# Queries and keys of three branches with stationary weights, differential values first, one division on VectorE: a hybrid encoder trunk on one core

## The chip, the cores and the metric

One core of a Trainium2 chip runs the whole program in one launch. The metric is the device time of one execution in microseconds (us). TensorE is PE in the profile, its weight load PEld, VectorE DVE, ScalarE ACT, GpSimd POOL and SyncE SP.

## The reference, cut

Two layers work on x of 256 tokens by 1024. One projection of the normalised x gives the inputs of four branches: a (mLSTM, 4 heads of 128, with a short convolution on queries and keys), b (grouped-query attention, 8 heads, 2 key heads), c (neighbourhood attention, 8 heads) and d (differential attention, 4 heads with two score maps each). A gated sum goes through an output projection, and a SwiGLU feed-forward network (FFN) of width 2816 follows.

```python
def hybrid_layer(x, ...):
    h = rms_norm(x, norm1_g)
    proj = jnp.einsum('bsd,de->bse', h, w_in)
    (aq, ak, av, ao, ag, bq, bk, bv, cq, ck, cv, dq, dk, dv, gl) = jnp.split(proj, points, axis=-1)
    y_a = mlstm_branch(aq, ak, av, ao, ag, a_conv_w, a_gate_bias, a_norm_g)
    y_b = gqa_branch(bq, bk, bv, b_qnorm_g, b_knorm_g)
    y_c = natten_branch(cq, ck, cv, c_rpb)
    y_d = diff_branch(dq, dk, dv, d_lq1, d_lk1, d_lq2, d_lk2, d_subln_g, lambda_init)
    g = jax.nn.sigmoid(gl.astype(F32)).reshape(bsz, s, N_BRANCH, D_MODEL)
    merged = (g[:, :, 0] * (y_a @ w_up_a) + g[:, :, 1] * (y_b @ w_up_b)
              + g[:, :, 2] * (y_c @ w_up_c) + g[:, :, 3] * (y_d @ w_up_d))
    x = x + merged.astype(dt) @ w_out
    h2 = rms_norm(x, norm2_g)
    ffn = (jax.nn.silu(h2 @ w_ffn_gate) * (h2 @ w_ffn_up)) @ w_ffn_down
    return x + ffn
```

## The kernel before, in words

**Arithmetic.** Every large product is three matmuls: operands are split into a high part (fp32r) and a low part (the rest), and high x high, high x low and low x high are summed in PSUM. `mm3` issues the three.

**Weights.** They come in units of two halves. A half is 128 partitions by 1024 columns (512 KB) and lies in one of four buffers `raw`. ACT copies its high part into one of five buffers `whi` (`emit_hi`), DVE subtracts to get the low part into `wlo` (`emit_lo`), and the next load is issued. `need_half(h, live)` makes sure that half h is converted before a block uses it; `live` is the oldest half still in use, and a conversion goes at most five halves beyond it.

**Blocks.** The list `PLAN` names the blocks of a layer in order: `d0 d1` (queries and keys of branch d, two heads' worth each), `a0 a1` and `c0 c1` alike, `dv av cv` values, `bkv` and `bq` for branch b, `ao` the output gate of a, `gXn` and `uXn` the merge gate and the up-projection of branch X, column half n. Nearly all of them go through `in512` and `blk512`: the transposed activations `xT` are stationary (128 tokens), 512 columns of weights move, and two token halves t use two of the three dense PSUM banks `pd`. So a block wants a half, does 12 matmuls with it (two t, two k tiles of 128, three products), and goes on to the next. `tok_evac` copies a finished bank to SBUF on ACT with the token's norm factor as scale per partition (`rc`, `r8`: columns of the statistics tile `st`). Since that result has tokens on partitions and the attention wants head dimensions there, `a_head` (one per head of a) and `soft_item` (one per pair of heads of b, c, d) first transpose it on PE, in four transposes for a, c and d (two for b), into a bank `pa` of five.

```python
            PS.put(p)
            yield
            while not (PS.ok(2) and W2.ok(2) and SM.ok(1) and B["ready"](i)):
                yield
            ps, e, sm = (PS.get(), PS.get()), (W2.get(), W2.get()), SM.get()
```

**Order.** Nothing is scheduled on the chip. `slot`, called between the matmul groups of a block, decides what is put next into the queues of the other engines: first evacuations (`later`), then conversions, then steps of the tasks (`a_head`, `soft_item` and others), as long as DVE and ACT are not more than `FILL` = 2.5 us ahead of PE by the planner's own costs (`Meter.cost`, `Track`). `until` holds the emission of a block up until a condition is met. So a changed block changes the place of conversions and small work in all queues.

**End of the FFN.** Of the last two units of the down projection, column chunk 0 is done for both t with both units, then chunk 1 (`pairs`, in the loop near the end of `trunk`); in the last layer the last quarter goes through `last_block` in two pieces of 256 columns.

Other names: `K4`, `W2`, `SM`, `RQ`, `RE`, `YT`, `T2`, `EA` are pools of tiles (k, w, sm, rq, re, yt, t, acc in the rows); `Res.ok(n)` asks for n free ones.

Of the kernel before, what the change touches and what calls it, by code (L numbers as in the profile page):

```python
# [15 lines left out]
ALU = mybir.AluOpType  # L16
# [21 lines left out]
PLAN = ("d0 d1 dv bkv a0 a1 av bq gd0 gd1 ud0 ud1 c0 c1 cv gb0 gb1 ub0 ub1 "  # L38
# [132 lines left out]
def trunk(ctx: ExitStack, tc, x_in, wts, par, parc, cst, dist, t2w, fg, out):  # L171
# [56 lines left out]
    mvt = sb("mvt", [128, 16])  # L228

    with tc.manual_schedule():  # L230
# [268 lines left out]
        bnd = {"i": 0, "sq": 0, "done": set()}  # L499
# [23 lines left out]
        def square(t, c, st):  # L523
            w = W2.get()
            A.activation(w[:, :512], x[:, t, c * 512:(c + 1) * 512], AF.Square,
                         accum_out=st[:, 2 * c + t:2 * c + t + 1])
            W2.put(w)
            bnd["sq"] += 1
            if bnd["sq"] % 4 == 0:
                V.tensor_tensor(st[:, 4:6], st[:, 0:2], st[:, 2:4], op=ALU.add)  # L530
                V.tensor_scalar(st[:, 4:6], st[:, 4:6], 1.0 / D, EPS, op0=ALU.mult, op1=ALU.add)
                rsq(st[:, 6:8], st[:, 4:6], 2)
                V.tensor_scalar(st[:, 8:10], st[:, 6:8], 0.5, None, op0=ALU.mult)
                V.tensor_tensor(st[:, 10:12], st[:, 6:8], st[:, 8:10], op=ALU.mult)
                for i in range(5):
                    V.tensor_scalar(st[:, 12 + 2 * i:14 + 2 * i], st[:, 6:8], 0.125 * 4 ** i, None, op0=ALU.mult)
# [128 lines left out]
        def a_head(B, h, pc):  # L665

            while not ("t%d" % (h // 2) in B and B["fly"] < 2 and PS.ok(1) and W2.ok(3)):
                yield
            B["fly"] += 1
            tok = B["t%d" % (h // 2)]  # L670
            p, xp, cv, th = PS.get(), W2.get(), W2.get(), W2.get()
# [4 lines left out]
            if h % 2 == 1:  # L676
                B["freet%d" % (h // 2)]()
            xv_ = xp[:, :512].rearrange("p (i n) -> p i n", i=2)
            yield
            A.activation(xp[:, :512], p, AF.Copy)  # L680
# [3 lines left out]
            for i in (0, 1):  # L684
                A.activation(cs_[i], p[:, i * 256:(i + 1) * 256], AF.Identity, scale=taps[i][1])
            PS.put(p)
# [11 lines left out]
            W2.put(xp, th)  # L698
# [101 lines left out]
        def soft_item(B, i, kind):  # L800
# [3 lines left out]
            while not (B["src"](i) is not None and PS.ok(1) and RQ.ok(1)):  # L804
                yield
            qs, ks, free = B["src"](i)
            p, r = PS.get(), RQ.get()
            for t in (0, 1):
                T.transpose(p[:, tsl(t)], qs(t), ident)
                if ks is not None:  # L810
                    T.transpose(p[:, 256 + t * 128:256 + (t + 1) * 128], ks(t), ident)
            free()
            n = 256 if ks is None else 512
            yield
            A.activation(r[:, 0, :n], p[:, :n], AF.Copy)
            yield
            sub_lo(r[:, 1, :n], p[:, :n], r[:, 0, :n])
            PS.put(p)
# [42 lines left out]
            if kind != "d":  # L861
                for c in (0, 1):
                    e3 = e[c][:, :512].rearrange("p (t n) -> p t n", t=2)
                    G.tensor_tensor(e3, e3, rz[:, 2 * c:2 * c + 2].unsqueeze(2).to_broadcast([128, 2, 256]),
                                    op=ALU.mult)
# [92 lines left out]
        def pair_src(B):  # L958

            def src(i):  # L960
                tl = B.get("t%d" % (i // 2))
                if tl is None:
                    return None

                def free():
                    B["used"] = B.get("used", 0) + 1
                    if B["used"] in (2, 4):
                        B["freet%d" % (B["used"] // 2 - 1)]()
                o = (i % 2) * 128
                return (lambda t: tl[:, t, o:o + 128]), (lambda t: tl[:, t, 256 + o:256 + o + 128]), free  # L970
            return src

        def d_main(l, B):
            li = 0.8 - 0.6 * math.exp(-0.3 * l)
            B["src"] = pair_src(B)
# [16 lines left out]
            while "t0" not in B:  # L992
                yield
# [20 lines left out]
        def b_main(B):  # L1014
# [53 lines left out]
            def src(i):  # L1068
# [3 lines left out]
                return (lambda t: qt_[:, t * 512 + i * 128:t * 512 + (i + 1) * 128]), None, free  # L1072
# [8 lines left out]
        def c_main(l, B):  # L1081
            B["t2"] = {}
            B["done"] = 0
            B["src"] = pair_src(B)
            B["ready"] = lambda i: i in B["t2"] and "vr" in B
            B["v"] = lambda kt, i, c: vc[:, kt, 2 * i + c]
            while "t0" not in B or not yt_ok("c"):
                yield
# [23 lines left out]
        for l in range(L):  # L1112
# [5 lines left out]
            r8 = lambda t, i=0, st=st: st[:, 12 + 2 * i + t:13 + 2 * i + t]  # L1118

            def tok_evac(B, key, tl=None, halves=False, early=False):  # L1120
                if tl is None:
                    res = EA if early else K4
                    until(lambda: res.ok(1))
                    raw_ = res.get()
                    B["free" + key] = lambda: res.put(raw_)
                    tl = raw_ if early else raw_.rearrange("p (t n) -> p t n", t=2)
# [3 lines left out]
                def done(t, p):  # L1130
                    if halves:
                        if B is Bd:

                            for i in (0, 1):
                                A.activation(tl[:, t, tsl(i)], p[:, tsl(i)], AF.Identity,
                                             scale=r8(t, 2 * int(key[1]) + i + 1))
                        else:
                            A.activation(tl[:, t, 0:256], p[:, 0:256], AF.Identity, scale=r8(t))
                        A.activation(tl[:, t, 256:512], p[:, 256:512], AF.Identity, scale=rc(t))
                    else:  # L1140
                        A.activation(tl[:, t, :], p, AF.Identity, scale=rc(t))
# [118 lines left out]
            for n in PLAN:  # L1260
                if n in start:
                    start[n]()
                if l == 0 and n == PLAN[0]:
                    first_block(tok_evac(Bs[n[0]], "t" + n[1], halves=n[0] != "a", early=n[0] != "c"),
                                pc[:, C_G1:C_G1 + 8])
# [8 lines left out]
                else:  # L1274
                    in512(n, tok_evac(Bs[n[0]], "t" + n[1], halves=n[0] != "a", early=n[0] != "c"))
# [147 lines left out]
            for c, t, un, j in ([(0, t, *q) for q in pairs for t in (0, 1)] + [(1, t, *q) for t in (0, 1) for q in pairs]):  # L1423
# [129 lines left out]
```

## Time and profile before

| | before |
|---|---|
| runs, median (lowest to highest) | 1070.75 us (1070.56 to 1071.57), 3 runs |
| the profiled execution, its own time | 1070.18 us |
| its span | 1068.4 us |
| granted TensorE clock, mean | 0.999 |
| matmuls on PE | 5270 |
| weight halves of 1024 columns (512 KB) | 331 loads |

The span is what the profiler saw between the first and last instruction; the execution's own time is 1.8 us longer. In the table of windows each stretch shows the busy time of every engine and, in brackets, its instructions; in a timeline the first number is the start from the span's start, the second the duration of the row, and x the instructions in it. Matmuls overlap, so the distance of two starts, and not the duration, tells what a matmul costs PE.

### The profile page before, as it was taken

Reading aid. Unit: us, or ns where it says so; the run is one execution under the profiler, and the core shown is the slowest. Engines: PE = TensorE matmul, PEld = TensorE weight load, DVE = VectorE, ACT = ScalarE, POOL = GpSimd, SP = SyncE. Lnnn points to the kernel's source line nnn. Section 1 sums busy time; section 2 is a strip of 40 time slices with the busy share of each in tenths; the row PEclk is TensorE's granted clock in tenths of the full one; section 3 lists DMA queues with packets and bytes.
Section 4 is the critical chain, followed back from the end, with each engine's and each line's share of the span. In section 5 each row is a group of like instructions: output and inputs, shape, how many; then the busy total and the mean of one; then the engine's idle time right before and its main releaser. Section 6 shows DMA issues by size and latency. Waiting matters only on the chain.

```text
span 1068.4 us, 14722 instructions
## 1 busy us (share of the span) xinstructions
PE 1055.5 (99%) x5270; PEld 876.2 (82%) x5270; DVE 760.6 (71%) x1356; ACT 617.3 (58%) x1091; POOL 156.3 (15%) x130
## 2 busy tenths in 40 slices
PE   9999999999999999999999999999999999999997
PEld 7888887888888888888788888788888888888885
DVE  5889798788656755565576989987975666556555
ACT  6766658775444544444468656687744464444443
POOL 0010345143300000000000006434223000000000
PEclk9999999999999999999999999999999999999999
DMA  8355434445555564555544444355465555564551
GB/s 300 122 178 176 158 134 155 161 146 188 191 181 169 197 203 171 197 185 185 185 160 143 164 168 150 126 169 170 136 199 194 181 172 202 174 210 164 197 191 65
DMA packets 53001, 184.80 MB, mean 173 GB/s; under 512 B 6081, under 2 KB 7489, under 8 KB 52929
## 3 DMA queue, kind: packets, MB, share of 16 engines
q1 hardware_dynamic: 50256, 178.33, 49.6%
q10 hardware_dynamic: 2672, 5.55, 1.7%
q8 instruction: 41, 0.67, 0.2%
q14 instruction: 32, 0.25, 0.1%
HBM read 182.80 MB, written 1.05 MB: 172 GB/s over the span
## 4 chain that ended last, share of the span: by engine, by line
PE 93%; DVE 5%; ACT 1%; issue 1%; DMA 0%; POOLq 0%; POOL 0%; DVEq 0%; ACTq 0%
PE pd L166 66%; PE pa L166 27%; DVE wlo L166 1%; DVE w L166 1%; DVE sm L166 1%; ACT w L166 1%; DVE k L166 1%; DMA x<-in_x_dram 0%; DVE rq L166 0%; ACT whi L166 0%; ACT yt L166 0%; DVE acc L166 0%; DVE yt L166 0%; ACT pa L166 0%; DVE x L166 0%
## 5 line engine op out<-in xcount | busy, mean ns | idle before, releaser
L166 PE MATMUL pd<-whi,xT 128*128 128x512 f32 (+1 forms) x1952 | 623.9, 391 | 0.0
L166 DVE TENSOR_TENSOR wlo<-raw,whi 128x1024 fp32r<-128x1024 f32 (+2 forms) x344 | 424.1, 1244 | 104.3 <-ACT whi L166 103.1
L166 ACT ACTIVATE whi<-raw 128x1024 fp32r<-128x1024 f32 (+2 forms) x344 | 354.6, 1040 | 140.2 <-PE pd L166 106.6
L166 PEld LDWEIGHTS pd<-whi,xT 128*128 128x128 f32 x1952 | 364.9, 188 | 74.0
L166 PE MATMUL pd<-wlo,xT 128*128 128x512 f32 (+1 forms) x976 | 377.6, 387 | 0.3 <-DVE wlo L166 0.3
L166 PEld LDWEIGHTS pd<-wlo,xT 128*128 128x128 f32 x976 | 183.5, 188 | 35.3 <-DVE wlo L166 1.4
L166 PE MATMUL pa<-whi,yt 128*128 128x512 f32 x408 | 137.0, 397 | 1.4 <-ACT yt L166 1.4
L166 PEld LDWEIGHTS pa<-whi,yt 128*128 128x128 f32 x408 | 76.5, 188 | 18.1 <-ACT yt L166 1.9
L166 PE MATMUL pd<-whi,yt 128*128 128x512 f32 (+1 forms) x272 | 86.2, 386 | 0.0
L166 PE MATMUL pa<-wlo,yt 128*128 128x512 f32 x204 | 79.5, 390 | 0.0
L166 POOL TENSOR_TENSOR st<-st,mhalf 128x2 f32<-128x2 f32 (+1 forms) x6 | 3.9, 656 | 513.9 <-DVE st L166 513.9
L166 DVE SCALAR_TENSOR_TENSOR w<-w,pd 128x256 f32<-128x256 f32 x44 | 18.6, 423 | 83.0 <-ACT w L166 82.8
L166 ACT ACTIVATE k<-pd,st 128x512 f32<-128x512 f32 (+1 forms) x52 | 31.6, 626 | 53.2 <-PE pd L166 53.0
L166 PEld LDWEIGHTS pd<-whi,yt 128*128 128x128 f32 x272 | 50.6, 188 | 9.7
L166 ACT ACTIVATE w<-pd,st 128x256 f32<-128x256 f32 (+1 forms) x48 | 23.7, 493 | 51.6 <-PE pd L166 51.6
L166 PE MATMUL pd<-wlo,yt 128*128 128x512 f32 (+1 forms) x136 | 52.2, 384 | 0.0
L166 ACT ACTIVATE yt<-pa 128x512 fp32r<-128x512 f32 x34 | 20.3, 598 | 55.0 <-PE pa L166 54.9
L166 PEld LDWEIGHTS pa<-wlo,yt 128*128 128x128 f32 x204 | 38.4, 188 | 7.3
L166 POOL TENSOR_TENSOR w<-w,sm 128x512 f32<-128x512 f32 x32 | 39.5, 1257 | 30.6 <-DVE sm L166 30.6
L166 POOL TENSOR_TENSOR acc<-acc,k 128x512 f32<-128x512 f32 x16 | 31.7, 1982 | 80.3 <-DVE k L166 80.3
L166 ACT ACTIVATE w<-w,sm 128x256 f32<-128x256 f32 x64 | 31.8, 502 | 14.8 <-DVE sm L166 9.4
L166 DVE TENSOR_TENSOR yt<-pa,yt 128x512 fp32r<-128x512 f32 x30 | 20.7, 690 | 27.0 <-ACT yt L166 26.9
(156 smaller groups left out, 1025.5 us busy)
## 6 DMA issues: line engine op xcount, KB each, us to landing
raw<-in_wts_dram SPq DMA_DIRECT2D x331, 512.0 KB, 3.7
t<-in_t2w_dram ACTq DMA_DIRECT2D x8, 384.0 KB, 3.6
raw<-in_wts_dram SPq DMA_DIRECT2D x8, 272.0 KB, 3.3
x<-in_x_dram ACTq DMA_DIRECT2D x4, 256.0 KB, 6.0
pt<-in_par_dram SPq DMA_DIRECT2D x1, 584.0 KB, 6.0
pt<-in_par_dram ACTq DMA_DIRECT2D x1, 584.0 KB, 5.0
out_dram<-k SPq DMA_DIRECT2D x2, 288.0 KB, 2.1
raw<-in_wts_dram SPq DMA_DIRECT2D x2, 256.0 KB, 4.7
```

The lines of the kernel that those rows point to most:

```text
L166: return f(out, *a, **k)
```

## The change

- `dv` is moved ahead of `d0 d1` in `PLAN`, and the five scaled copies of the norm factor leave `st` (five small products on DVE a norm).
- The blocks `d0 d1 a0 a1 c0 c1` go through a new `qk_block`: weights are stationary (128 columns), all 256 tokens of `xT` move, so the result has head dimensions on partitions. Four column groups (0, 2, 1, 3) run one after another, each over all eight k tiles; DVE writes the finished group to SBUF, multiplied by a row of norm factors (`rrow`, made once a norm by two matmuls in `row_scale`).
- `a_head` and `soft_item` of c and d lose their four transposes and read that tile. `soft_item` of b keeps two.
- The division by the softmax sum of branch b goes from POOL (two products of 512) to DVE (four of 256). Branch c's stays on POOL.
- At the end of the FFN chunk (1, 0) is put ahead of the last unit of chunk 0.

```diff
-PLAN = ("d0 d1 dv bkv a0 a1 av bq gd0 gd1 ud0 ud1 c0 c1 cv gb0 gb1 ub0 ub1 "
+PLAN = ("dv d0 d1 bkv a0 a1 av bq gd0 gd1 ud0 ud1 c0 c1 cv gb0 gb1 ub0 ub1 "
...
-                for i in range(5):
-                    V.tensor_scalar(st[:, 12 + 2 * i:14 + 2 * i], st[:, 6:8], 0.125 * 4 ** i, None, op0=ALU.mult)
+                if bnd["i"] % 2 == 1:
+                    tasks.append(row_scale(st))
...
+            for t in (0, 1):
+                T.matmul(p[:, tsl(t)], st[:, 6 + t:7 + t].to_broadcast([128, 128]), ident, start=True, stop=True)
+            yield
+            A.activation(rrow, p[:, 0:S], AF.Copy)
+            PS.put(p)
+            bnd["row"] = bnd["i"]
...
-            while not ("t%d" % (h // 2) in B and B["fly"] < 2 and PS.ok(1) and W2.ok(3)):
+            while not (h in B and B["fly"] < 2 and W2.ok(2)):
...
-            for i in (0, 1):
-                for t in (0, 1):
-                    o = i * 256 + (h % 2) * 128
-                    T.transpose(p[:, i * 256 + t * 128:i * 256 + (t + 1) * 128], tok[:, t, o:o + 128], ident)
...
+            if kind == "b":
...
+            else:
+                while not (i in B and RQ.ok(1)):
+                    yield
+                (qk, free), r = B[i], RQ.get()
+                A.activation(r[:, 0, :], qk, AF.Copy)
+                yield
+                sub_lo(r[:, 1, :], qk, r[:, 0, :])
+                free()
...
+                    for qt in (0, 1):
+                        q2 = slice(qt * 256, (qt + 1) * 256)
+                        V.tensor_scalar(e[c][:, q2], e[c][:, q2], rz[:, 2 * c + qt:2 * c + qt + 1], None, op0=ALU.mult)
...
+            def qk_block(n):
...
+                def done(col, p):
+                    i, k = col % 2, col // 2
+                    item = 2 * int(n[1]) + i
+                    o = tl[:, i, k * S:(k + 1) * S]
+                    f = 1.0 if k else {"a": 1.0, "c": 0.125, "d": 0.125 * 4.0 ** (item + 1)}[n[0]]
+                    if f == 1.0:
+                        V.tensor_tensor(o, p[:, 0:S], rrow, op=ALU.mult)
+                    else:
+                        V.scalar_tensor_tensor(o, p[:, 0:S], f, rrow, op0=ALU.mult, op1=ALU.mult)
...
+                u0, u1 = Unit("in", n, 0), Unit("in", n, 1)
+                for ci, col in enumerate((0, 2, 1, 3)):
+                    p = bank()
+                    for kt in range(8):
+                        if kt % 2 == 0:
+                            need_half(2 * u0.u + kt // 2, 2 * u0.u + (kt // 2 if ci == 3 else 0))
+                        for t in (0, 1):
+                            x_ready(t, kt // 4)
+                        w = (u0, u1)[kt // 4].get(kt % 4 * 512 + col * 128, 128)
+                        T.matmul(p[:, 0:S], w[0], xT[:, 0, kt, :], start=kt == 0, stop=False)
+                        T.matmul(p[:, 0:S], w[0], xT[:, 1, kt, :], start=False, stop=False)
+                        T.matmul(p[:, 0:S], w[1], xT[:, 0, kt, :], start=False, stop=kt == 7)
+                        if kt == 7:
+                            until(lambda: bnd["row"] == bnd["i"])
+                            later(lambda col=col, p=p: done(col, p))
+                        if kt % 4 == 3:
+                            slot()
...
-                    in512(n, tok_evac(Bs[n[0]], "t" + n[1], halves=n[0] != "a", early=n[0] != "c"))
+                    qk_block(n)
...
-            for c, t, un, j in ([(0, t, *q) for q in pairs for t in (0, 1)] + [(1, t, *q) for t in (0, 1) for q in pairs]):
+            for c, t, un, j in ([(c, t, *pairs[0]) for c, t in ((0, 0), (0, 1), (1, 0))]
+                                + [(c, t, *pairs[1]) for c, t in ((0, 0), (0, 1), (1, 0))] + [(1, 1, *q) for q in pairs]):
```

In the rows that follow, `whi_72` to `whi_76` and `wlo_77` to `wlo_81` are the five buffers of the weight ring, `raw_111` to `raw_114` the four raw ones; `pd` are dense banks, `pa` the other PSUM banks, `rq` query tiles and `kb` keys of branch b, `k`, `w` and `sm` pool tiles, `acc` the merged sum.

PE at the start of `c0` in layer 0, as it was: one half (`whi_76`, `wlo_81`) is used for both t before the next, and score products of branch b lie between.

```order
L166 MATMUL pd_61<-whi_75,yt_83 128x512
L166 MATMUL pd_62<-whi_76,xT 128x512
L166 MATMUL pd_62<-wlo_81,xT 128x512
L166 MATMUL pd_62<-whi_76,xT 128x512 x2
L166 MATMUL pd_62<-wlo_81,xT 128x512
L166 MATMUL pd_62<-whi_76,xT 128x512
L166 MATMUL pa_64<-kb,rq_87 128x256
L166 MATMUL pd_63<-whi_76,xT 128x512
L166 MATMUL pa_65<-ident,k_1_99 128x128 x2
L166 MATMUL pd_62<-whi_72,xT 128x512
```

PE at the same place now: the end of `ud1`, then the first column group of `c0`.

```order
L166 MATMUL pd_63<-whi_75,yt_83 128x512
L166 MATMUL pd_61<-xT,whi_76 128x256 x2
L166 MATMUL pd_61<-xT,wlo_81 128x256
L166 MATMUL pd_61<-xT,whi_76 128x256 x2
L166 MATMUL pd_61<-xT,wlo_81 128x256
L166 MATMUL pd_61<-xT,whi_72 128x256 x2
L166 MATMUL pd_61<-xT,wlo_77 128x256
L166 MATMUL pd_61<-xT,whi_73 128x256 x2
L166 MATMUL pd_61<-xT,wlo_78 128x256
L166 MATMUL pd_61<-xT,whi_74 128x256 x2
L166 MATMUL pd_61<-xT,wlo_79 128x256
L166 MATMUL pa_67<-ident,k_1_99 128x128 x2
```

The first column group reads four halves (76, 72, 73, 74) one after another, and the second begins again with `whi_76`; before, the second half was read only after both t of the first.

DVE around the same place, as it was (`mvt` and `bsm` belong to branch b's normalisation).

```order
L166 TENSOR_SCALAR k_2_100<-k_2_100,mvt,sm_123 128x128 x4
L166 TENSOR_TENSOR wlo_79<-raw_114,whi_74 128x1024
L166 TENSOR_SCALAR k_2_100<-k_2_100,mvt,sm_123 128x128 x4
L166 TENSOR_REDUCE sm_124<-pa_67 128x2
L166 SCALAR_TENSOR_TENSOR sm_124<-sm_124,bsm 128x2
L166 TENSOR_REDUCE sm_119<-pa_64 128x2
L166 SCALAR_TENSOR_TENSOR sm_119<-sm_119,bsm 128x2
L166 TENSOR_TENSOR wlo_80<-raw_111,whi_75 128x1024
L166 RECIPROCAL sm_124<-sm_124 128x4
L166 TENSOR_TENSOR rq_86<-pa_65,rq_86 128x256
L166 RECIPROCAL sm_119<-sm_119 128x4
L166 TENSOR_TENSOR wlo_81<-raw_112,whi_76 128x1024
```

DVE there now.

```order
L166 TENSOR_TENSOR wlo_78<-raw_113,whi_73 128x1024
L166 TENSOR_SCALAR k_3_101<-k_3_101,mvt,sm_123 128x128 x4
L166 TENSOR_REDUCE sm_119<-pa_66 128x2
L166 SCALAR_TENSOR_TENSOR sm_119<-sm_119,bsm 128x2
L166 SCALAR_TENSOR_TENSOR acc_97<-k_0_98,pd_63 128x512
L166 TENSOR_SCALAR k_3_101<-k_3_101,mvt,sm_123 128x128 x4
L166 RECIPROCAL sm_124<-sm_124 128x4
L166 TENSOR_SCALAR w_1_103<-w_1_103,sm_124 128x256 x2
L166 TENSOR_SCALAR w_7_109<-w_7_109,sm_124 128x256 x2
L166 TENSOR_TENSOR wlo_79<-raw_114,whi_74 128x1024
L166 TENSOR_TENSOR wlo_80<-raw_111,whi_75 128x1024
```

Between the conversions into `wlo_78` and `wlo_79`, which the first column group of `c0` both wants, now stand two normalisations of four, two pairs of reductions, an accumulation, a reciprocal and the four new divisions.

PE at the end of the FFN of the last layer, as it was: the transposes of the last chunk, then the first use of `yt_85`, which holds that chunk.

```order
L166 MATMUL pa_64<-whi_74,yt_84 128x512
L166 MATMUL pa_66<-ident,w_4_106 128x128 x4
L166 MATMUL pa_67<-whi_75,yt_85 128x512
L166 MATMUL pa_67<-wlo_80,yt_85 128x512
L166 MATMUL pa_67<-whi_75,yt_85 128x512
```

PE there now.

```order
L166 MATMUL pa_65<-whi_74,yt_84 128x512
L166 MATMUL pa_67<-ident,w_6_108 128x128 x4
L166 MATMUL pa_66<-whi_73,yt_84 128x512
L166 MATMUL pa_66<-wlo_78,yt_84 128x512
L166 MATMUL pa_66<-whi_73,yt_84 128x512
L166 MATMUL pa_66<-whi_74,yt_84 128x512
L166 MATMUL pa_66<-wlo_79,yt_84 128x512
L166 MATMUL pa_66<-whi_74,yt_84 128x512
L166 MATMUL pa_68<-whi_75,yt_85 128x512
L166 MATMUL pa_68<-wlo_80,yt_85 128x512
```

Six matmuls on the chunk before (`yt_84`) now stand between the transposes and the first use of `yt_85`.

## Rows read from the trace of the kernel before

**Rows 1.** The page, part 1: busy us, share of the span, instructions

```profile
PE 1055.5 (99%) x5270; PEld 876.2 (82%) x5270; DVE 760.6 (71%) x1356; ACT 617.3 (58%) x1091; POOL 156.3 (15%) x130
```

**Rows 2.** The page, part 4: the chain that ended last, by engine

```profile
PE 93%; DVE 5%; ACT 1%; issue 1%; DMA 0%; POOLq 0%; POOL 0%; DVEq 0%; ACTq 0%
```

**Rows 3.** Waits of PE for other engines: us in total, times, longest us

```profile
PE pa L166 <- DVE rq L166: 2.1, 2, 1.6
PE pd L166 <- POOL ident masks.py:199: 1.5, 1, 1.5
PE pa L166 <- ACT yt L166: 1.4, 2, 0.7
```

**Rows 4.** Windows, two attention stages: length, PE, PEld, DVE, ACT, POOL, clock, DMA, GB/s

```profile
20.00:240.00 220.00, 218.62 (x1224) 182.52 (x1223) 187.42 (x430) 157.43 (x340) 57.51 (x49) 1.00 0.47 158
...
536.00:770.00 234.00, 232.38 (x1291) 194.29 (x1290) 199.24 (x451) 163.93 (x350) 60.42 (x50) 1.00 0.46 155
```

**Rows 5.** Timeline of PE in the last FFN: start, us, engine, operation

```profile
1042.11 0.39 PE L166 MATMUL pd<-wlo,xT 128*128 128x512 f32 x1
1042.34 0.62 PE L166 MATMUL pd<-whi,xT 128*128 128x512 f32 x2
1042.79 0.39 PE L166 MATMUL pd<-wlo,xT 128*128 128x512 f32 x1
```

**Rows 6.** Timeline of PE in the last block, 256 columns each

```profile
1058.98 0.28 PE L166 MATMUL pd<-wlo,yt 128*128 128x256 f32 x1
1059.10 0.40 PE L166 MATMUL pd<-whi,yt 128*128 128x256 f32 x2
1059.34 0.28 PE L166 MATMUL pd<-wlo,yt 128*128 128x256 f32 x1
```

**Rows 7.** Timeline of PE at the end of the first layer's FFN

```profile
524.62 0.60 PE L166 MATMUL pa<-ident,w 128*128 128x128 f32 x4
525.90 0.50 PE L166 MATMUL pa<-whi,yt 128*128 128x512 f32 x1 [0.69 <-ACT yt L166]
526.24 0.40 PE L166 MATMUL pa<-wlo,yt 128*128 128x512 f32 x1
526.63 0.73 PE L166 MATMUL pa<-whi,yt 128*128 128x512 f32 x2
...
529.04 0.60 PE L166 MATMUL pa<-ident,x 128*128 128x128 f32 x4
529.40 0.48 PE L166 MATMUL pa<-whi,yt 128*128 128x512 f32 x1
```

**Rows 8.** Timeline of DVE in several stretches of layer 0

```profile
25.84 3.49 DVE L166 TENSOR_TENSOR wlo<-raw,whi 128x1024 fp32r<-128x1024 f32 x3
...
45.72 0.42 DVE L166 CUSTOM_DVE_ANT_0 w<-pa,ndist 128x256 f32<-128x256 f32 x1
...
47.48 0.72 DVE L166 TENSOR_TENSOR wlo<-raw,whi 128x544 fp32r<-128x544 f32 x1
...
58.02 0.23 DVE L166 SCALAR_TENSOR_TENSOR gtok<-pd,st,pt 128x16 f32<-128x16 f32 x1
...
60.40 1.22 DVE L166 TENSOR_TENSOR wlo<-raw,whi 128x1024 fp32r<-128x1024 f32 x1
...
145.43 0.68 DVE L166 SCALAR_TENSOR_TENSOR acc<-k,pd 128x512 f32<-128x512 f32 x1
...
155.57 1.11 DVE L166 TENSOR_SCALAR k<-k,mvt,sm 128x128 f32<-128x128 f32 x4
...
158.75 0.69 DVE L166 TENSOR_REDUCE sm<-pa 128x2 f32<-128x512 f32 x1
159.48 0.16 DVE L166 SCALAR_TENSOR_TENSOR sm<-sm,bsm 128x2 f32<-128x2 f32 x1
159.56 0.68 DVE L166 TENSOR_REDUCE sm<-pa 128x2 f32<-128x512 f32 x1
```

**Rows 9.** Groups by form: count | busy us, mean ns | idle before, releaser

```profile
L166 DVE SCALAR_TENSOR_TENSOR w<-pd,st,w 128x256 f32<-128x256 f32 x44 | 21.3, 484 | 1.6
L166 DVE TENSOR_SCALAR w<-w,sm 128x256 f32<-128x256 f32 x16 | 5.6, 348 | 0.0
L166 POOL TENSOR_TENSOR w<-w,sm 128x512 f32<-128x512 f32 x32 | 39.5, 1257 | 30.6 <-DVE sm L166 30.6
L166 ACT ACTIVATE whi<-raw 128x1024 fp32r<-128x1024 f32 x328 | 344.9, 1059 | 140.1 <-PE pd L166 106.6 <-PE pa L166 22.5 <-DMA raw<-in_wts_dram 4.0
```

**Rows 10.** Timeline of PE in c0 of layer 0: scores of branch b

```profile
163.45 0.97 PE L166 MATMUL pa<-kb,rq 64*128 64x256 f32 x11 [0.31 <-ACT w L166]
```

**Rows 11.** The chain in order of time, at the end of bkv

```profile
54.90 3.04 PE pd L166 x24
```

More of the change, by code (lines that the diff above doesn't have):

```diff
@@ L498, in trunk @@
         stats = [sb("st%d" % i, [128, 22]) for i in range(2)]
-        bnd = {"i": 0, "sq": 0, "done": set()}
+        bnd = {"i": 0, "sq": 0, "row": 0, "done": set()}
         def boundary_chunk(t, c, gcol, st):
@@ L684, in a_head @@
             for i in (0, 1):
-                A.activation(cs_[i], p[:, i * 256:(i + 1) * 256], AF.Identity, scale=taps[i][1])
-            PS.put(p)
+                A.activation(cs_[i], xv_[:, i, :], AF.Identity, scale=taps[i][1])
             yield
@@ L803, in soft_item @@
             slope = 4.0 ** (-1 - i) if kind == "d" else 1.0
-            while not (B["src"](i) is not None and PS.ok(1) and RQ.ok(1)):
-                yield
[L806 to L818, printed above, removed]
+            if kind == "b":
+                while not (PS.ok(1) and RQ.ok(1)):
+                    yield
+                qs, free = B["src"](i)
+                p, r = PS.get(), RQ.get()
+                for t in (0, 1):
+                    T.transpose(p[:, tsl(t)], qs(t), ident)
+                free()
+                yield
+                A.activation(r[:, 0, :S], p[:, :S], AF.Copy)
+                yield
+                sub_lo(r[:, 1, :S], p[:, :S], r[:, 0, :S])
+                PS.put(p)
+            else:
+                while not (i in B and RQ.ok(1)):
+                    yield
+                (qk, free), r = B[i], RQ.get()
+                A.activation(r[:, 0, :], qk, AF.Copy)
+                yield
+                sub_lo(r[:, 1, :], qk, r[:, 0, :])
+                free()
             yield
@@ L1071, in free @@
                         K4.put(qt_)
-                return (lambda t: qt_[:, t * 512 + i * 128:t * 512 + (i + 1) * 128]), None, free
+                return (lambda t: qt_[:, t * 512 + i * 128:t * 512 + (i + 1) * 128]), free
             B["src"] = src
@@ L1117, in trunk, with free @@
             rh = lambda t, st=st: st[:, 8 + t:9 + t]
-            r8 = lambda t, i=0, st=st: st[:, 12 + 2 * i + t:13 + 2 * i + t]
-            def tok_evac(B, key, tl=None, halves=False, early=False):
-                if tl is None:
[L1122 to L1126, printed above, removed]
+            def qk_block(n):
+                B, res = Bs[n[0]], (K4 if n[0] == "c" else EA)
+                until(lambda: res.ok(1))
+                raw_ = res.get()
+                tl = raw_.rearrange("p (i n) -> p i n", i=2) if n[0] == "c" else raw_
+                used = []
+                def free():
+                    used.append(1)
+                    if len(used) == 2:
+                        res.put(raw_)
+                def done(col, p):
[7 more added lines that the diff above has]
+                        V.scalar_tensor_tensor(o, p[:, 0:S], f, rrow, op0=ALU.mult, op1=ALU.mult)
+                    if k:
+                        B[item] = tl[:, i, :], free
+                u0, u1 = Unit("in", n, 0), Unit("in", n, 1)
[4 more added lines that the diff above has]
+                            need_half(2 * u0.u + kt // 2, 2 * u0.u + (kt // 2 if ci == 3 else 0))
+                        for t in (0, 1):
+                            x_ready(t, kt // 4)
[8 more added lines that the diff above has]
+                            slot()
@@ L1127, in tok_evac @@
+            def tok_evac(B, key, tl=None):
+                if tl is None:
+                    until(lambda: K4.ok(1))
+                    raw_ = K4.get()
+                    tl = raw_.rearrange("p (t n) -> p t n", t=2)
                 else:
@@ L1130, in done @@
                 def done(t, p):
[L1131 to L1141, printed above, removed]
+                    A.activation(tl[:, t, :], p, AF.Identity, scale=rc(t))
                     if t == 1:
@@ L1263, in trunk @@
                 if l == 0 and n == PLAN[0]:
[L1264 to L1265 removed]
+                    first_block(evacs[n](), pc[:, C_G1:C_G1 + 8])
                 elif n in special:
```

41 lines of the change are left out of this document (13 added, 28 removed).

## The prediction

> **What bounds the kernel now.** I read the page's busy times first, then the chain, then who made TensorE wait, then the stages, then single stretches. The reader should see one engine that never rests. PE is busy for 1055.5 of 1068.4 us [rows 1] and the chain that ended last runs through it for 93% [rows 2]. Its waits for another engine are few: 2.1 us (twice, for the low half of a query tile), 1.5 us once at the very start and 1.4 us (twice, for the last FFN chunk) are the longest sums [rows 3]. No wait of size for a weight conversion stands there. So the time is TensorE's columns, and a change pays only by taking columns away or loses by making PE wait. VectorE is the engine that could make it wait: in the two attention stages it works 187.42 of 220 us and 199.24 of 234 us [rows 4].
>
> **PE's own work.** Before, a block of queries and keys is 48 matmuls of 512 columns; three start in 1042.79 - 1042.11 = 0.68 us [rows 5], 0.227 us each, so 10.9 us. Now it is 96 of 256 columns; three start in 1059.34 - 1058.98 = 0.36 us [rows 6], 0.120 us each, so 11.5 us. The same columns cost 0.63 us more per block because the part of a matmul that does not scale is paid twice. Twelve blocks (six a layer) give **+7.5 us**. Removed are 24 groups of four transposes (8 d items, 8 c items, 8 a heads over both layers); four cost 529.40 - 529.04 = 0.36 us on PE [rows 7], so **-8.6 us**. The new row of scales is two f32 matmuls of 128 columns a layer; at the transposes' 0.09 to 0.12 us that is **+0.4 us**. PE's work alone changes by -0.7 us.
>
> One sentence apart: the Trainium skill (TensorE: Matmul & The Clock Gate, Back-to-back issue gap) gives N/2.4 + 2.5 ns, estimated 109 ns at 256 and 216 at 512, which would make the twelve blocks +1.5 us and the whole sum 6 us lower; the rows show 120 and 227 ns, so the sum stays with them.
>
> **End of the FFN.** Before, PE issues four transposes, then waits for ACT's and DVE's copies of the last chunk: 525.90 - (524.62 + 0.36) = 0.92 us, and 0.16 us more for the low half, since 0.39 us instead of 0.23 us pass from 526.24 to 526.63 [rows 7]. Both layers show it (1.4 us for two waits in the profile's own count [rows 3]). Now one more group of six matmuls, 6 x 0.227 = 1.36 us, stands between the transposes and the first use. It covers 1.08 us whole: **-2.2 us** for two layers.
>
> **The weight ring, where I see the loss.** Weights arrive as halves of 1024 columns, go through ACT (high part) and DVE (low part) into a ring of five buffers. A 512-column block takes one half every 12 x 0.227 = 2.72 us. A new block runs its first column group over all eight k tiles, so it wants four halves in 4 x 0.72 = 2.9 us, and keeps four of five buffers until its last column group. DVE makes one in 3.49/3 = 1.16 us [rows 8]. So the ring can no longer lend ahead, and whatever DVE has queued between two conversions lands on PE. The order shows what is queued; the rows give the times. Per start:
> - **gate-up block to c0.** After the scores of the first grouped-query item, DVE has 4 pairs of reduction and small product at 159.56 - 158.75 = 0.81 us, one conversion, 8 normalisations at 1.11/4, an accumulation of some 0.6 us, a reciprocal of about 0.1 us (the small product takes 0.16 us), the four new divisions, and the conversion wanted [rows 8]. A division is not in the trace on VectorE; the nearest row is the 0.348 us TENSOR_SCALAR of 256 [rows 9]. Together 3.2 + 1.2 + 2.2 + 0.6 + 0.1 + 1.4 + 1.2 = 9.9 us. PE has from there 6 + 6 matmuls of 512 (2.7 us), twelve score matmuls of about 1.0 us (eleven took 0.97 us [rows 10]), two transposes (0.2 us) and three halves (2.2 us): 6.1 us. PE waits **3.7 us**.
> - **bkv to a0.** The last d item's softmax pass, 47.48 - 45.72 = 1.76 us, ends some 0.4 us after bkv (its scores stand 12 x 3.04/24 = 1.5 us before bkv's end [rows 11]); then gates and values, 60.40 - 58.02 = 2.4 us [rows 8]; then two conversions. The first is ready at 0.4 + 2.4 + 1.2 = 4.0 us and wanted after two halves, at 1.4 us; the second comes 1.16 us later and is wanted 0.72 us later, 0.4 us more: **3.0 us**.
> - **d0 to d1.** One softmax pass (1.76 us), one evacuation (0.35 us, as the pass over 256 elements takes [rows 9]), two conversions (2.3 us): 4.4 us and a hop of 0.2 us, against five halves of PE work, 3.6 us: **1.0 us**.
> - **a0 to a1, c0 to c1.** The same count leaves **0.6 us** and **0.4 us**.
> - **dv to d0.** In layer 0 the block starts at once where before d1 took its halves over 10.9 us; three more conversions, 3.5 us, of which PE's first half hides 0.7, and a hop of 0.2 us: **3.0 us**. In layer 1 three halves are ahead and only the fourth, behind the scale statistics that POOL returns, is late: **1.0 us**.
>
> That is 11.7 us in layer 0 and 9.7 us in layer 1, **+21.4 us**. Of the old waits of this stage [rows 3] I give back 1.5 us, because the queues are drained whenever PE waits.
>
> **Edits that I cost at nothing.** ACT loses the evacuations and the copies before the convolution; it is no bound. DVE gains 48 evacuations of 256 elements at up to 0.484 us and 32 divisions at 0.348 us, and loses ten small ones: about 33 us, beside 32.6 us and 34.8 us that it is idle in the two stages [rows 4, 9]. It is in the waits above where it stands before a conversion; elsewhere PE's weight work covers it. If that cover fails, it is the third rival. POOL's 1.257 us products for the grouped-query items [rows 9] go; nobody on the path waits for them. With dv first its values only lie ready earlier.
>
> The sum against the profiled execution (1070.18 us, 0.57 us under the median of 1070.75, 1.8 us of it outside the span): -0.7 - 2.2 + 21.4 - 1.5 = +17.0, so 1087.2, against the median **1088 us**.
>
> Bounds of the waits. Below: if DVE had nothing else queued, a block that follows a block still waits about 0.4 us for the ring (buffer free at 0.72, high part 1.06 [rows 9], three conversions 3.5, against 5.0 us), 2.4 us over six such starts. Above: each start also meets a backlog of one more softmax pass, 1.76 x 12 = 21 us more, from which I take the middle part only. I take the counted queue, since it is fixed by the order and not by how far DVE is ahead.
>
> **Rivals.**
> 1. *The conversions keep up, and columns decide* (ends faster). The mechanism is the drop of transposes and the FFN order; it decides if DVE reaches each conversion before PE needs it, that is if the queued work at every start is under PE's 3.6 to 6 us. For it: before, nothing waits for a conversion [rows 3]. Against it: that was with one half in 2.72 us. Time: 1070.75 - 0.7 - 2.2 = 1067.9 us. Chance 0.18.
> 2. *Only the ring's own limit shows.* The planner's tasks stand behind, not before, the conversions on the chip. 1067.9 + 2.4 = 1070.3, up to 1073 us. Chance 0.12.
> 3. *VectorE becomes the bound of both attention stages.* Its 33 us more lie half on the path beside the counted waits: 1088 + 16 = 1104 us. For it: it is 85% busy there [rows 4]. Against it: after each wait of PE it has caught up. Chance 0.10.
> The forecast keeps 0.60.
>
> **How the numbers follow.** About 0.2%, 2.1 us, is what a measurement of this kernel tells from no change. Rival 1 is faster by more than that: 0.18. Rival 2 lies about it: 0.10 the same and 0.02 slower. The forecast and rival 3 are slower, with rival 2's rest: 0.72. The forecast's own range, with half and with one and a half of its 21.4 us of waits, is 1077 to 1099 us. The whole range leaves out rival 3 and the forecast's upper end (some 0.05) and reaches down to rival 1, since its 0.18 beside them would be too much to leave out: 1067 to 1100 us.
>
> **What would show it.** Right: PE waits for DVE's low halves (and ACT's high ones) come to some 20 us in the list of waits, in groups at the first column group of the twelve blocks, the longest at c0; matmuls of 256 columns start every 0.12 us; the waits of about 0.9 us at the end of both FFNs are gone. Wrong: if those starts show less than 5 us in all, the step from the order to the waits fails; if the 256-column matmuls start further apart than 0.127 us, weight loading costs more than the tail of before shows; if PE waits mostly in mid-block for a free bank, the evacuations and not the conversions are late.

## The result and the profile after

The changed kernel takes 1099.98 us (median of 4 runs, 1098.82 to 1101.96) against 1070.65 us for the kernel before on the same chips: ratio 1.027, 95% interval 1.0256 to 1.0284. It is 29.3 us slower. Forecast were 1088 us and a range of 1067 to 1100, so the sign and the mechanism were right and the size was too small: the time lies 0.02 us under the upper end of the range and above the forecast's own 1077 to 1099 us. (The prediction's "gate-up block to c0" is the step from `ud1`, the second up-projection block of branch d, to `c0`.)

The page of the kernel after, busy times and chain by engine:

```profile
PE 1066.2 (97%) x5758; PEld 908.2 (83%) x5758; DVE 786.8 (72%) x1416; ACT 596.3 (54%) x1037; POOL 145.7 (13%) x114
...
PE 83%; DVE 10%; ACT 4%; issue 2%; DMA 1%; POOL 0%; SPq 0%; POOLq 0%; DVEq 0%; ACTq 0%
```

PE's share of the chain falls from 93% [rows 2] to 83%, and DVE's rises from 5% to 10%. DVE's busy time grows by 26.2 us [rows 1]; the prediction counted 33 (an evacuation takes 0.42 us and not 0.484, and twenty small products are gone, not ten). The waits of PE, kernel after (us in total, times, longest):

```profile
PE pd L166 <- DVE wlo L166: 18.7, 15, 3.8
PE pd L166 <- POOL ident masks.py:199: 1.5, 1, 1.5
PE pa L166 <- POOL st L166: 1.3, 1, 1.3
PE pa L166 <- ACT w L166: 0.9, 2, 0.4
```

Low halves (`wlo`) were not among the first three waits before [rows 3]; now they are 18.7 us in 15 waits. The largest is at `c0`. PE there, in layer 0 (timeline: start, us, operation, idle time before):

```profile
170.59 0.40 PE L166 MATMUL pd<-xT,whi 128*128 128x256 f32 x2
174.77 0.38 PE L166 MATMUL pd<-xT,wlo 128*128 128x256 f32 x1 [3.78 <-DVE wlo L166]
```

And DVE in the same time:

```profile
165.25 0.69 DVE L166 TENSOR_REDUCE sm<-pa 128x2 f32<-128x512 f32 x1
...
166.85 1.23 DVE L166 TENSOR_TENSOR wlo<-raw,whi 128x1024 fp32r<-128x1024 f32 x1
167.99 1.11 DVE L166 TENSOR_SCALAR k<-k,mvt,sm 128x128 f32<-128x128 f32 x4
...
170.61 0.68 DVE L166 SCALAR_TENSOR_TENSOR acc<-k,pd 128x512 f32<-128x512 f32 x1
171.21 1.11 DVE L166 TENSOR_SCALAR k<-k,mvt,sm 128x128 f32<-128x128 f32 x4
172.24 0.17 DVE L166 RECIPROCAL sm<-sm 128x4 f32<-128x4 f32 x1
172.44 1.14 DVE L166 TENSOR_SCALAR w<-w,sm 128x256 f32<-128x256 f32 x4
173.50 2.36 DVE L166 TENSOR_TENSOR wlo<-raw,whi 128x1024 fp32r<-128x1024 f32 x2
```

DVE never rests between the first reduction at 165.25 and the wanted conversion, which ends at about 173.50 + 1.2 = 174.7: 9.4 us, where the prediction counted 9.9.

At `d0` of layer 0 the picture is another one. DVE is idle before each conversion, because ACT's high part is not there, and ACT has waited for the load of the fourth half:

```profile
23.34 1.06 ACT L166 ACTIVATE whi<-raw 128x1024 fp32r<-128x1024 f32 x1 [1.59 <-DMA raw<-in_wts_dram]
24.43 1.23 DVE L166 TENSOR_TENSOR wlo<-raw,whi 128x1024 fp32r<-128x1024 f32 x1 [0.74 <-ACT whi L166]
25.71 0.39 PE L166 MATMUL pd<-xT,wlo 128*128 128x256 f32 x1 [0.76 <-DVE wlo L166]
```

What the prediction had no term for stands in the windows. Five stretches of the kernel after (length, PE, PEld, DVE, ACT, POOL, granted clock, DMA share, GB/s):

```profile
26.00:33.00 7.00, 5.75 (x28) 5.46 (x28) 2.38 (x8) 2.43 (x7) 0.71 (x1) 0.51 0.42 142
70.00:74.00 4.00, 3.51 (x17) 3.51 (x18) 3.44 (x8) 3.20 (x11) 0.00 (x0) 0.57 0.57 176
176.00:180.00 4.00, 4.00 (x27) 3.55 (x26) 2.31 (x8) 0.21 (x1) 0.00 (x0) 0.57 0.73 251
609.00:614.00 5.00, 4.84 (x28) 4.63 (x27) 3.87 (x13) 2.73 (x13) 0.00 (x0) 0.66 0.79 267
712.00:719.00 7.00, 5.96 (x32) 5.51 (x33) 4.15 (x10) 0.38 (x1) 0.00 (x0) 0.51 0.44 150
```

Around and after the waits at `d0` (layer 0), `a0` and `c0` (both layers) the granted clock is 0.5, that is 1.2 GHz instead of 2.4. What it costs shows in one timeline of PE, where the clock comes back:

```profile
29.60 0.63 PE L166 MATMUL pd<-xT,whi 128*128 128x256 f32 x2
30.03 0.41 PE L166 MATMUL pd<-xT,wlo 128*128 128x256 f32 x1
30.24 0.63 PE L166 MATMUL pd<-xT,whi 128*128 128x256 f32 x2
...
33.07 0.28 PE L166 MATMUL pd<-xT,wlo 128*128 128x256 f32 x1
33.19 0.40 PE L166 MATMUL pd<-xT,whi 128*128 128x256 f32 x2
33.42 0.28 PE L166 MATMUL pd<-xT,wlo 128*128 128x256 f32 x1
```

Three matmuls of 256 columns take 30.24 - 29.60 = 0.64 us from start to start at half clock and 33.42 - 33.07 = 0.35 us at the full one.

The end of the FFN, kernel after, layer 0 (PE): the transposes are followed at once by matmuls, where 0.92 us passed before [rows 7].

```profile
542.53 0.60 PE L166 MATMUL pa<-ident,w 128*128 128x128 f32 x4
542.88 0.48 PE L166 MATMUL pa<-whi,yt 128*128 128x512 f32 x1
543.20 0.39 PE L166 MATMUL pa<-wlo,yt 128*128 128x512 f32 x1
```

### The profile page after: what moved, and what is told of

Read it like the earlier page. It is cut to its first block, busy times and chain, and to the rows that moved or that the text cites. A ratio compares the mean times of both kernels' runs of the same rounds, so it can differ in the third digit from the quotient of the medians.

```text
span 1098.1 us, 15683 instructions
## 1 busy us (share of the span) xinstructions
PE 1066.2 (97%) x5758; PEld 908.2 (83%) x5758; DVE 786.8 (72%) x1416; ACT 596.3 (54%) x1037; POOL 145.7 (13%) x114
## 4 chain that ended last, share of the span: by engine, by line
PE 83%; DVE 10%; ACT 4%; issue 2%; DMA 1%; POOL 0%; SPq 0%; POOLq 0%; DVEq 0%; ACTq 0%
PE pd L166 60%; PE pa L166 23%; DVE wlo L166 3%; DVE w L166 3%; ACT w L166 2%; DVE sm L166 1%; DMA raw<-in_wts_dram 1%; ACT whi L166 1%; DVE k L166 1%; DVE acc L166 0%; DVE rq L166 0%; ACT k L166 0%; DVE re L166 0%; ACT pa L166 0%; DVE mvt L166 0%
## 5 line engine op out<-in xcount | busy, mean ns | idle before, releaser
L166 PE MATMUL pd<-whi,xT 128*128 128x512 f32 (+1 forms) x1568 | 494.1, 388 | 0.0
L166 PEld LDWEIGHTS pd<-whi,xT 128*128 128x128 f32 x1568 | 292.9, 188 | 58.8
L166 PE MATMUL pd<-wlo,xT 128*128 128x512 f32 (+1 forms) x784 | 302.5, 386 | 0.0
L166 PEld LDWEIGHTS pd<-wlo,xT 128*128 128x128 f32 x784 | 147.4, 188 | 28.1 <-DVE wlo L166 0.3
L166 PE MATMUL pd<-xT,whi 128*128 128x256 f32 x768 | 148.0, 293 | 0.7 <-ACT whi L166 0.7
L166 PE MATMUL pd<-xT,wlo 128*128 128x256 f32 x384 | 113.2, 295 | 18.7 <-DVE wlo L166 18.7
L166 PEld LDWEIGHTS pd<-xT,whi 128*128 128x128 f32 x768 | 124.0, 198 | 2.0 <-ACT whi L166 0.9
L166 PEld LDWEIGHTS pd<-xT,wlo 128*128 128x128 f32 x384 | 76.3, 199 | 21.8 <-DVE wlo L166 21.8
L166 ACT ACTIVATE k<-pd,st 128x512 f32<-128x512 f32 x36 | 24.7, 685 | 58.4 <-PE pd L166 58.1
```

What stands on the lines that cost most here:

```text
L166: return f(out, *a, **k)
```

## The experiments

**Is it the ring?** `halves` keeps every matmul and all work of the other engines, and changes the order inside the block: all four column groups on one half before the next, in four PSUM banks.

```diff
-                for ci, col in enumerate((0, 2, 1, 3)):
-                    p = bank()
-                    for kt in range(8):
...
+                until(lambda: PS.ok(2))
+                ps = {0: bank(), 1: bank(), 2: PS.get(), 3: PS.get()}
...
+                for half in (0, 1):
+                    need_half(2 * u0.u + half, 2 * u0.u + half)
+                    for i in (0, 1):
+                        for col in (i, i + 2):
+                            for kt in (2 * half, 2 * half + 1):
+                                mms(col, kt)
+                        slot()
```

> The changed kernel with one edit: the block of queries and keys goes through its weights half by half, all four column groups on each half (24 matmuls of 256 columns, 2.9 us), instead of one column group over all four halves. Same matmuls, same work on VectorE and ScalarE. Theory (the loss is the ring: four halves wanted in 2.9 us, so what VectorE has queued lands on PE, and the clock falls after the long waits): the waits for low halves at the starts of these blocks (18.7 us) shrink to under 3 us, the clock stays at 1.00, and the time is 1067 to 1070 us. Rival (VectorE is simply the bound with its extra work): the work is the same, so the time stays above 1090 us. Rival (256-column matmuls with stationary weights cost more than their 0.120 us): PE's own work grows, time 1075 us or more without waits.

Measured: 1088.44 us, ratio 1.0161 (1.0143 to 1.018). The waits of PE in it:

```profile
PE pa L166 <- ACT w L166: 5.3, 2, 2.6
PE pd L166 <- DVE vb L166: 4.8, 2, 2.4
PE pa L166 <- DVE k L166: 4.2, 2, 2.4
PE pa L166 <- ACT re L166: 1.7, 2, 0.9
```

The low halves are gone from the list, and 11.5 us with them: the demand of four halves at once made those waits. But the time is not 1068. PE now meets the next thing that is late: softmax work of branch b, and the bank that `bkv`'s gates and values leave. Two stretches of half clock stay in each layer. The theory held for the conversions and failed for the total.

`pairs` is a dose between: two groups at a time over all four halves, then the other two (`for i in (0, 1)` over `ps = (bank(), bank())`, with `need_half` at each half).

> A dose between the two: two column groups go together over all four halves, then the other two, so four halves are wanted in 5.8 us. Theory: per start PE has 2.2 us more before the fourth half: c0 3.9 to about 1.7 us, a0 3.2 to about 1.5 us, d0 of layer 0 2.8 to under 1 us, d1 and c1 none, together some 7 to 9 us of waits in place of 22; few or no stretches at half clock. Time 1074 to 1082 us. Rival (VectorE bound): above 1090 us.

Measured: 1093.19 us, ratio 1.0206 (1.0173 to 1.0239). Low halves are 10.3 us, longest 2.8, so the dose works on the conversions as counted; again what is saved there (8.4 us) comes back as waits on `re`, `vb` and `acc` (11.4 us together). What this run gains goes with the clock: three stretches at half clock, 10.2 us in all, instead of five with 23.9 us.

**Does the clock cost anything of its own?** `warm` gives PE something to do while it would wait.

```diff
                     p = bank()
+                    if ci == 0 and n in ("a0", "c0"):
+                        for _ in range(15):
+                            nc.tensor.matmul(p[:, 0:128], ident, ident, start=True, stop=True)
```

> The changed kernel with 15 extra matmuls on the identity (into a bank that is overwritten afterwards) ahead of a0 and c0 in both layers; all other engines have the same order. They fill about 3.4 us, about what PE waits there. Theory (after a wait of over 3 us PE runs at half clock for several us): these four waits are filled instead of idle, the clock stays full there, and 8.4 us come back: 1091 to 1093 us. Rival (the half clock is a record of the waits and costs nothing beside them): 1100 us or slower by what exceeds the waits, up to 1102 us.

Measured: 1093.55 us, ratio 1.021 (1.0193 to 1.0227), 6.4 us less than the changed kernel by the two ratios. The windows at `a0` and `c0`, layer 0 and then layer 1:

```profile
70.00:75.00 5.00, 4.90 (x42) 4.70 (x41) 4.93 (x13) 4.42 (x16) 0.00 (x0) 1.00 0.47 177
172.00:180.00 8.00, 7.58 (x68) 7.11 (x67) 7.18 (x18) 2.57 (x8) 0.00 (x0) 1.00 0.41 133
608.00:614.00 6.00, 6.00 (x54) 6.00 (x53) 5.55 (x26) 3.13 (x12) 0.00 (x0) 1.00 0.65 228
708.00:716.00 8.00, 7.56 (x68) 7.09 (x67) 7.14 (x17) 3.03 (x10) 0.00 (x0) 1.00 0.47 143
```

The clock is full in all four places and the time falls although PE does 60 matmuls more. The half clock is a cost beside the waits. Compared matmul by matmul, the four stretches lose 1.2, 1.5, 1.6 and 2.6 us in the changed kernel against `warm`, besides the waits. (1.0 us of the missing 2 is the wait for `st` in layer 0, 2.4 us here instead of 1.3.)

**Is it the division?** `bpool` puts branch b's division back on POOL in the changed kernel (`if kind != "d":` in place of `if kind == "c":`).

> The changed kernel with branch b's division back on GpSimd, everything else as changed. Theory: the four divisions (1.14 us) leave VectorE's queue ahead of the late half of c0, so that wait falls from 3.9 to about 2.8 us in each layer, -2.3 us, and up to 4.5 us more where the clock then stays up: 1093 to 1098 us. Rival (VectorE bound in both stages): 18 us of VectorE work go and the time falls by more than 8 us. Rival (the division is hidden): 1100 us.

Measured: 1098.63 us, ratio 1.0263 (1.0239 to 1.0288), which includes the changed kernel's. The wait at `c0` only falls from 3.94 to 3.68 us (start to start, beyond the usual 0.12). DVE, POOL and PE there:

```profile
171.33 0.39 DVE L166 TENSOR_TENSOR rq<-pa,rq 128x256 fp32r<-128x256 f32 x1
171.64 4.01 DVE L166 TENSOR_TENSOR wlo<-raw,whi 128x1024 fp32r<-128x1024 f32 x2
```

```profile
171.55 3.02 POOL L166 TENSOR_TENSOR w<-w,sm 128x512 f32<-128x512 f32 x2 [7.87 <-DVE sm L166]
```

```profile
169.81 0.40 PE L166 MATMUL pd<-xT,whi 128*128 128x256 f32 x2
173.73 0.39 PE L166 MATMUL pd<-xT,wlo 128*128 128x256 f32 x1 [3.52 <-DVE wlo L166]
```

Counted from the block's first matmul (167.44 here, 168.45 in the changed kernel) DVE reaches the conversion after 4.20 us instead of 5.05. But this conversion and the one after it take 4.01 us together, where the changed kernel's two take 2.36. POOL's two division products run at the same time and take 1.04 and 2.02 us, where the next two take 1.04 each. The high part is not what is late: PE has used it from 169.81 on. In this run the 266 conversions of 1024 columns that no POOL work overlaps take 1.23 us at most; the wanted one takes 2.04, in layer 1 as well. So what leaves DVE's queue comes back as a longer conversion beside POOL's products. That the products lengthen it is read from this overlap; no run separates it from everything else. `bdve` is the same edit alone, in the kernel before:

> The kernel before with only branch b's division moved to VectorE. Theory: before, one half is wanted every 2.7 us, VectorE has room, and the 11 us more of it cost nothing: within 1 us of 1070.65. Rival (VectorE is already the bound in the stage of b and c): 3 to 9 us slower.

Measured: 1070.32 us, ratio 0.999 (0.9979 to 1.0). No cost where a half is wanted every 2.7 us.

**Does the wait go when its cause does?** `bkvlate` emits `bkv`'s evacuations one slot later, so that two conversions for `a0` stand ahead of them.

```diff
-                                later(lambda t=t: done(t, ps[t]))
+                                later(lambda t=t: done(t, ps[t]), 2)
```

> The changed kernel with one number edited: bkv's evacuations (gates and values, 2.4 us on VectorE with two waits for ScalarE in them) are emitted one slot later, so the third and fourth conversion of a0 stand ahead of them. Theory (what VectorE has queued ahead of a wanted conversion lands on PE one for one): a0's wait falls from 3.2 + 0.3 to about 1.2 us in each layer, some 0.5 us come back at the bank that the evacuations free later, and the half clock after a0 may go (1.8 to 2 us a layer): 1092 to 1097 us. Rival (the conversions wait for their high parts or their ring buffers anyway): the wait at a0 stays above 2.5 us and the time within 1 us of the changed kernel.

Measured: 1107.88 us, ratio 1.0346 (1.0329 to 1.0362); the changed kernel, run `again` beside it, 1100.15 us, ratio 1.0274 (1.0258 to 1.0289).

> The changed kernel once more, unedited, beside the next two on the same chip: 1099 to 1101 us, with the same five stretches at half clock.

PE in `bkvlate` at `a0` and at the start of `a1`, layer 0:

```profile
71.93 0.39 PE L166 MATMUL pd<-xT,wlo 128*128 128x256 f32 x1 [0.16 <-DVE wlo L166]
...
73.12 0.50 PE L166 MATMUL pd<-xT,whi 128*128 128x256 f32 x2 [0.45 <-DVE vb L166]
...
85.83 0.38 PE L166 MATMUL pd<-xT,wlo 128*128 128x256 f32 x1 [0.81 <-DVE wlo L166]
...
88.25 0.39 PE L166 MATMUL pd<-xT,wlo 128*128 128x256 f32 x1 [1.45 <-DVE wlo L166]
```

At `a0` it does what was expected: 3.2 us become 0.3 at the conversion and 0.6 at the bank (start to start), and the half clock there is gone. Then `a1`, which had no such wait, gets 1.0 + 1.6 us, and `c1` a wait of 2.8 us for a high part from ACT. The wait at `a0` follows from the queue, as counted; but the waits for weight halves, low and high, do not shrink in sum: 23.5 us against 19.5 in `again`. Another 1.5 us is the wait for POOL's `st` in layer 0. Why `c1`, a hundred us later, changes was not traced.

`first` takes that further, with two edits at once: conversions are emitted ahead of everything, and a ring buffer counts as free as soon as its last matmul is emitted.

```diff
+            while not forced and state["lo"] < min(nhalf, state["live"] + NH):
+                emit_hi()
+                emit_lo()
             now = [p for p in pending if p[0] <= 0]
```

> The changed kernel with conversions put ahead: at every slot all conversions that the ring has room for are emitted before evacuations and task steps, and the planner counts a half as free as soon as its last matmul is emitted. The blocks still want four halves in 2.9 us. Theory (it is the place of the conversions behind softmax work in VectorE's and ScalarE's queues that PE pays): the waits for low halves fall from 18.7 us to under 7 us and the half clock goes, while softmax work that comes later makes PE wait elsewhere for up to 8 us: 1074 to 1084 us. Rival (the ring alone sets it: four halves cannot be made in 2.9 us whatever is queued): the waits stay above 14 us, 1092 us or more.

Measured: 1154.99 us, ratio 1.0788 (1.0757 to 1.0818). Waits of PE:

```profile
PE pa L166 <- DVE re L166: 15.0, 17, 2.4
PE pd L166 <- ACT whi L166: 12.7, 4, 5.7
PE pa L166 <- POOL st L166: 6.4, 2, 5.7
PE pd L166 <- DVE vb L166: 6.3, 2, 3.7
PE pd L166 <- DVE wlo L166: 5.0, 11, 0.8
```

Low halves fall to 5.0 us, as expected, but PE waits elsewhere for far more than the 8 us allowed: for softmax work that matmuls in its queue behind the blocks need, for `st`, and 5.7 us each for two high parts at `c0`. PE is at half clock for 65 us, against 24 in the changed kernel.

**What is left in the half-by-half form?** `halves_bpool` is `halves` with branch b's division on POOL; `actevac` is that with the 48 evacuations on ACT, which leaves out the norm factor of these queries and keys.

```diff
-                        V.scalar_tensor_tensor(o, p[:, 0:S], f, rrow, op0=ALU.mult, op1=ALU.mult)
+                    A.activation(o, p[:, 0:S], AF.Copy, scale=f)
```

> The half-by-half block (1088 us) with branch b's division back on GpSimd. There PE waited for softmax work and not for conversions, 17 us more than before, with VectorE busy without a gap from 150 to 182 us. Theory (in that form VectorE's added work is the bound of those stretches): 2.3 us of VectorE per b item go, and of the two starts of c0 (13 us of waits and half clock) at least 5 us come back: 1078 to 1084 us. Rival (the order of PE's queue and its banks, not the amount of VectorE's work): 1087 to 1090 us.

> The half-by-half block with branch b's division on GpSimd (1083 us), and the 48 evacuations of query and key groups on ScalarE with a constant scale instead of on VectorE with the row of norm factors; the norm factor of these queries and keys is left out. VectorE then has about the work of before. Theory (what is left, 12 us over before, is VectorE's added work): 16 us of it go and the time comes to 1070 to 1076 us. Rival (the order of PE's queue and its banks): 1080 us or more.

Measured: 1083.01 us, ratio 1.0102 (1.0078 to 1.0125), and 1091.49 us, ratio 1.019 (1.0175 to 1.0206). The division is worth 5 to 6 us here, where PE waits for softmax work and no longer for the ring. But the amount of DVE's work is not what is left: over the whole run of `actevac`,

```profile
PE 1064.1 (98%) x5758; PEld 910.1 (84%) x5758; DVE 766.4 (70%) x1336; ACT 612.7 (56%) x1085; POOL 154.5 (14%) x130
```

DVE works 766.4 us, near before's 760.6 [rows 1] and 14 us less than in `halves_bpool` (780.7), and the kernel is slower than `halves_bpool`. ACT works 14 us more, so the run does not show what the lighter DVE alone is worth. Its waits are for ACT's, POOL's and DVE's softmax steps, with half clock from about 174 to 184 us after them. That the order and the latency of those steps decide there is the likely reading, not a shown one: which of them would have to move was not tried.

**The parts alone, on the kernel before.** `ffn` has only the new order at the end of the FFN, `dvfirst` only `dv` ahead of `d0 d1`.

> The kernel before with only the new order at the end of the FFN. Theory: the two waits of 0.85 us and the late low half go, 2.2 us: 1068.4 us against 1070.65. Rival (the copies of the last chunk are late in another place): 1070 to 1071 us.

> The kernel before with only the differential values moved ahead of the queries and keys in the list of blocks. Theory (no cost by itself; it costs only through what d0 then wants at once): within 2 us of before, 1069 to 1073 us. Rival (the later softmax of branch d makes PE wait by itself): 3 us or more slower.

Measured: `ffn` 1068.81 us, ratio 0.9981 (0.9969 to 0.9992), a gain of 2.0 us and the fastest kernel of this study. `dvfirst` 1075.22 us, ratio 1.0043 (1.0029 to 1.0057): 4.3 us slower, the rival's case. Its waits of PE:

```profile
PE pa L166 <- ACT acc L166: 3.3, 4, 1.4
PE pd L166 <- POOL ident masks.py:199: 1.5, 1, 1.5
PE pa L166 <- ACT yt L166: 1.4, 2, 0.7
```

With `dv` first, only the short `bkv` lies between `d1` and its transposes, which reach PE before ACT has copied `d1`; the clock is at half from 48.9 to 52.3 us after that. In the changed kernel those transposes are gone, so this cost can't simply be added to it.

## Why the prediction was right, and why it was too small

The gap of 29.3 us, by the start-to-start distance of every matmul in the two traces against what is usual for its shape:

| term | predicted, us | measured, us |
|---|---|---|
| PE's own work | -0.7 | -0.3 |
| end of the FFN | -2.2 | -1.7 (`ffn` alone -2.0) |
| starts, layer 0: `d0`, `d1`, `a0`, `a1`, `c0`, `c1` | 3.0, 1.0, 3.0, 0.6, 3.7, 0.4 | 2.8, 1.1, 3.2, 0, 3.9, 0.8 |
| starts, layer 1, same order | 1.0, 1.0, 3.0, 0.6, 3.7, 0.4 | 0.8, 1.1, 3.5, 0, 3.9, 0.8 |
| old waits given back | -1.5 | -1.0 |
| wait for the row of norm factors, layer 0 | none | +1.6 |
| other new waits (three places a layer) | none | +2.8 |
| half clock | none | about +9 |
| remainder | none | -3 |
| sum | +17.0 | +29.3 |

- **Columns.** Right. Three matmuls of 256 columns take 0.35 to 0.36 us from start to start, and twelve blocks cost what the tail of before let expect. The Trainium skill (TensorE: Matmul & The Clock Gate, Back-to-back issue gap) gives N/2.4 + 2.5 ns for single matmuls without their weight loads, which is an estimated 109 ns at 256 columns; the trace shows 120, after as before, and the measurement decides.
- **The ring.** Right in place and in sum: 21.4 us predicted, 21.9 measured, in the same five of six places. `halves` shows that the cause is the demand for four halves at once. `a0` to `a1` had enough cover. The counted mechanism, work in DVE's queue ahead of the conversion, holds at `d1`, `a0` and `c0`: 15.4 us predicted, 16.7 measured. At `d0` and `c1` (4.8 predicted, 5.2 measured) the agreement is luck: DVE is idle there, for 0.74 us before the last conversion of `d0` in layer 0 and for 1.25 us before the one that `c1` waits for, until ACT's high part comes, and at `d0` ACT has waited 1.59 us for the load. The hop of 0.2 us in two of the counts is in no run: PE starts 0.05 us after the conversion that it waits for. At `c0`, 9.9 - 6.1 is 3.8 and not 3.7.
- **The step that failed** is the end of the sum: waits were priced at their own length. After some of them PE works at half clock, which costs about 9 us in all (6.9 at `a0` and `c0` against `warm`, some 2 at `d0`). `warm` shows it by itself: same order, same lateness, clock full, 6.4 us less. The Trainium skill (TensorE: Matmul & The Clock Gate, HAM oscillation — how this bites in real kernels) says that a PE that waits long between pieces of work starts the next piece at half clock; the trace agrees at `a0` (0.50 from 71 to 73 us), but at `c0` of layer 0 PE comes back at the full clock and falls 1.4 us later. The cost should have been a term.
- **The row of norm factors.** Its two matmuls were priced at 0.4 us of PE. In layer 0 they stand in PE's queue before POOL's result is there: 1.6 us, and 1.9 to 3.4 us in `again`, `warm`, `bpool` and `bkvlate`, whose order is the same up to there.
- **"With dv first its values only lie ready earlier"** was wrong as a statement on that edit: alone it costs 4.3 us.
- **The rivals.** The first (conversions keep up) is refuted by the 18.7 us. The third (VectorE bounds the stages) named 1104 us, closer to the time than the forecast, but by another mechanism: `halves`, with the same work on DVE, is 11.5 us faster. Something of it is true: when the conversions no longer wait (`halves`) or are put first (`first`), PE waits for softmax work instead.
- **The range.** That 1099.98 us lies inside it is luck: `again` is at 1100.15, and the half clock and the other new waits, 13 us that no term stood for, were covered only by the width that was meant for the waits of the ring.
- **Where the expected gain is.** Even with every wait gone the blocks save 0.3 us of PE; what the change gains is the FFN's 2 us, which `ffn` has alone.

## What to carry to other kernels

Before a loop order is turned around, count how fast it asks for its operands and what stands in the producers' queues ahead of them: that count, from rows of the old trace, gave 15.4 of 16.7 us where the queue was what was late. Count every producer of the operand, though: in two of five places the high part or its load was late, and not the queue that was counted. Then add what a wait costs after its end, since PE came back at half speed from several of them. And mending one late operand in a static order of queues moved the wait to the next block here; compare the sum over the stage, not the place.

## What was not expected of the hardware

The clock did not follow the length of one wait: after 3.78 us at `c0` in layer 0 PE ran 1.4 us at full clock before it fell, in layer 1 it fell during the wait, and in `halves_bpool` a wait of 2.64 us before `c0` went with half clock in layer 1 (692 to 699 us) and not in layer 0; in `dvfirst` it fell after a wait of 1.37 us. The stretches at half clock lasted 3.4 to 6.8 us in the changed kernel. The wait for POOL's `st` varied from 1.3 to 3.1 us between kernels with the same order up to that place.

DVE's conversions were longer beside POOL's work: in the trace of the kernel before, 272 conversions of 1024 columns that overlapped none took 1.23 us at most, and of the 56 that did, 23 took over 1.3 us, up to 2.33. So a product that is moved to POOL need not be free for DVE, as `bpool` shows at `c0`.
